# A two-layer hybrid trunk: SwiGLU in products of 256 columns, other TensorE work between k tiles, and attention's values moved beside the recurrence's products

## The chip, the cores and the metric

The kernel runs on one core of one Trainium2 chip. The metric is the device time of one launch in microseconds (us); the time before is the median of three runs. A profile of one execution is read beside it. Five engines work in parallel, each through its own queue in order: TensorE (PE in the profile; its weight loads are PEld), VectorE (DVE), ScalarE (ACT), GpSimd (POOL) and SyncE (SP, which only issues the transfers here).

## The reference, cut to what matters

Two layers, 256 tokens, width 1024, all in float32:

```
h = rms_norm(x, norm_mix);  z = h @ w_in        # 4768 columns, split in nine parts
y_a = latent attention(z parts) @ w_proj_a      # 8 heads, causal, two blocks of 128 queries
y_b = gated linear recurrence(z parts) @ w_proj_b   # 4 heads, 128 x 128
x = x + (sigmoid(g_a) * y_a + sigmoid(g_b) * y_b) @ w_out
h = rms_norm(x, norm_ffn)
x = x + (silu(h @ w_gate) * (h @ w_up)) @ w_down    # 2816 wide
```

## The kernel before, in words

The activations lie transposed: 128 channels in the partitions, 256 tokens along the columns. Each float32 operand of a large product is split in two parts of type float32r, a high one and the rest (`split`, L207). A product of two split operands is three products on TensorE: high by high, high by low, low by high (low by low is left out). A **k tile** is one slice of 128 of the sum, that is, three such products which add into one PSUM tile.

There are two ways to write a k tile. `mm3` (L217) issues three products of 256 columns, at L227 (weights' high part by the activations' high part), L228 and L229. SwiGLU uses `mmw` (L231): one product of 512 columns, the weights' high part by the activations' high and low part side by side (L235), and one of 256 columns, the weights' low part by the activations' high part (L236). `mmw` leaves two sums in the two halves of a PSUM tile, so ScalarE copies one half (L862) and VectorE adds the other (L863) before the row scale is multiplied in (L864). For each of the 22 tiles of SwiGLU's width there are 2 x 8 k tiles (gate and up), and for each of the 8 output tiles 22 k tiles (down): 528 k tiles a layer, 1056 in all.

The weights come in chunks of about 1 MB in the order of `chunk_plan` (L46). `load` (L105) issues the transfer from SP's queue, ScalarE rounds it to the high part (L118), VectorE or now and then GpSimd makes the low part (L120), two chunks ahead of use.

Attention's two generators and the recurrence give small products in plain float32: transposes of heads (L482), scores (L570), transposes of the probabilities (L591), values (L597), the recurrence's products (L674, L696, L712, L780) and its transposes (L724); the norms' sums over tokens (L257) and the row scales (L275) are plain float32 too. They are issued from generators: the loop at L799 to L804 calls `next(at, ...)` and `next(rec, None)` ahead of each chunk of the input projection. In the program as written, one call of `attention()` (L602) does the scores of one step and the transposes and values of the step before. The order on each engine is then made by a scheduler that simulates a timeline and takes, among instructions that are ready by it, those of higher priority first; so it can place a small product in the middle of another tile's k tile where the k tile's next product is, by its own clock, not first in line.

Of the kernel before, what the change touches and what calls it, by code (L numbers as in the profile page):

```python
# [9 lines left out]
F32 = mybir.dt.float32  # L10
# [5 lines left out]
ALU = mybir.AluOpType  # L16
AX = mybir.AxisListType

P = 128
T = 256  # L20
TT = T // P
D = 1024
KD = D // P
L = 2
NH, NOPE, ROPE, VD = 8, 64, 32, 64
# [57 lines left out]
def trunk(ctx: ExitStack, tc: tile.TileContext, x_in, w_in, vec_in, gqk_in, cst_in, msk_in, out):  # L83
    nc = tc.nc
    V, S, G, PE = nc.vector, nc.scalar, nc.gpsimd, nc.tensor
# [6 lines left out]
    acc = ctx.enter_context(tc.tile_pool(name="acc", bufs=2, space=bass.MemoryType.PSUM))  # L92
    prj = ctx.enter_context(tc.tile_pool(name="prj", bufs=2, space=bass.MemoryType.PSUM))
    trp = ctx.enter_context(tc.tile_pool(name="trp", bufs=2, space=bass.MemoryType.PSUM))
    hgp = ctx.enter_context(tc.tile_pool(name="hgp", bufs=2, space=bass.MemoryType.PSUM))
# [107 lines left out]
    def bc(ap, shape):  # L203
        return ap.broadcast_to(shape)
# [11 lines left out]
    def mm3(ps, pairs, late=False, opens=True, closes=True):  # L216
        n = len(pairs)  # L217
        if late:
            for i, ((ah, al), (bh, bl)) in enumerate(pairs):
                PE.matmul(ps, ah, bh, start=i == 0, stop=False)  # L220
                PE.matmul(ps, ah, bl, start=False, stop=False)
            for i, ((ah, al), (bh, bl)) in enumerate(pairs):
                PE.matmul(ps, al, bh, start=False, stop=i == n - 1)
            return
        shared = not (opens and closes)
        for i, ((ah, al), (bh, bl)) in enumerate(pairs):
            PE.matmul(ps, ah, bh, start=opens and i == 0, stop=False, skip_group_check=shared)  # L227
            PE.matmul(ps, ah, bl, start=False, stop=False, skip_group_check=shared)  # L228
            PE.matmul(ps, al, bh, start=False, stop=closes and i == n - 1, skip_group_check=shared)  # L229

    def mmw(ps, items):  # L231

        n = len(items)
        for i, ((ah, al), b) in enumerate(items):
            PE.matmul(ps, ah, b, start=i == 0, stop=False)  # L235
            PE.matmul(ps[:, 0], al, b[:, 0], start=False, stop=i == n - 1)  # L236

    def squares(src, kt, both=False):

# [43 lines left out]
    def norm_in(l, col):  # L283

        xx = lay.tile([P, KD, 2, T], F32R, name="xx")
        xh, xl = xx[:, :, 0], xx[:, :, 1]
        for k in range(KD):
            split(xh[:, k], xl[:, k], xT[:, k], vec[:, l, col + k:col + k + 1])
        r, _, ps = norm_rows(token_stats(xT, KD, both=True))
        return xx, xh, xl, r, norm_cols(ps)  # L290
# [25 lines left out]
    for l in range(L):  # L316
# [248 lines left out]
        def scores(t, h0, hb):  # L565
            ns = (t + 1) * P
            ps = prj.tile([P, 512], F32, name="prj")
            pv = ps.rearrange("p (h s) -> p h s", s=ns)
            for h in range(hb):
                PE.matmul(pv[:, h], qT[:, h0 + h, t * P:(t + 1) * P], kT[:, h0 + h, :ns], start=True, stop=True)  # L570
            V.tensor_tensor(pv[:, :, t * P:], pv[:, :, t * P:], bc(cmask.unsqueeze(1), [P, hb, P]), ALU.add)
            mx = wk.tile([P, 4], F32, name="mx")
            V.tensor_reduce(mx[:, :hb], pv, AX.X, ALU.max)
            nb = wk.tile([P, 4], F32, name="nb")
            V.tensor_tensor(nb[:, :hb], mx[:, :hb], nsc[:, t, h0:h0 + hb], ALU.mult)
            pr = wk.tile([P, 512], F32, name="pr")
            sm = wk.tile([P, 4], F32, name="sm")
            prv = pr.rearrange("p (h s) -> p h s", s=ns)
            for h in range(hb):
                S.activation(prv[:, h], pv[:, h], AF.Exp, bias=nb[:, h:h + 1], scale=sc[:, t, h0 + h:h0 + h + 1], accum_out=sm[:, h:h + 1])  # L580
            rs = wk.tile([P, 4], F32, name="rs")
            V.reciprocal(rs[:, :hb], sm[:, :hb])
            for h in range(hb):
                S.activation(prv[:, h], prv[:, h], AF.Identity, scale=rs[:, h:h + 1])
            return pr

        def values(t, h0, hb, pr, po):

            pt = trp.tile([P, 512], F32, name="trp")
            for c in range(4):  # L590
                PE.transpose(pt[:, c * P:(c + 1) * P], pr[:, c * P:(c + 1) * P], ident)  # L591
            pT = wk.tile([P, 4, P], F32, name="pT")
            S.copy(pT, pt.rearrange("p (c s) -> p c s", c=4))
            for h in range(0, hb, 2):
                for s in range(t + 1):
                    for u in range(2):
                        PE.matmul(po[u * VD:(u + 1) * VD, (h0 + h) // 2], av[:, s, h0 + h + u], pT[:, (h + u) * (t + 1) + s], start=s == 0, stop=s == t)  # L597

        def attn_out(t, po):
            split(ah[:, :, t * P:(t + 1) * P], al[:, :, t * P:(t + 1) * P], po)  # L600

        def attention():  # L602
            prev = None
            for t in range(TT):
                hb = 4 // (t + 1)
                po = None
                for h0 in range(0, NH, hb):
                    cur = (t, h0, hb, scores(t, h0, hb))
                    if prev:
                        values(*prev)  # L610
                        if prev[0] != t:
                            attn_out(prev[0], prev[4])
                    if po is None:
                        po = trp.tile([P, 512], F32, name="trp").rearrange("p (c s) -> p c s", c=4)
                    prev = cur + (po,)
                    yield
            values(*prev)
            attn_out(prev[0], prev[4])
            yield

# [167 lines left out]
        for ci in (3, 4):  # L790
# [3 lines left out]
            if ci == 4:  # L794
                next(at)
        tchunk(5)
        tchunk(6)
        next(at)
        for ci in [0] + list(range(7, 17)):  # L799
            if ci in (8, 10, 12, 14):  # L800
                next(at, None)
            next(rec, None)
            if ci == 0:
                hchunk(0)  # L804
            else:
                tchunk(ci)
            if ci == 8:
                for h in range(HH):
                    th = wk.tile([P, T], F32, tag="w1", bufs=3, name="thg")
                    S.activation(th, sg[:, h], AF.Tanh, scale=0.5)  # L810
                    V.scalar_tensor_tensor(sg[:, h], th, 1.0, sg[:, h], ALU.add, ALU.mult)
# [35 lines left out]


        xx, xh, xl, r, rb = norm_in(l, V_FFN)
        ffp = tc.alloc_tile_pool(name=f"ffn{l}", bufs=1)  # L850
        ff2 = ffp.tile([P, KF, 2, T], F32R, name="ff2")
        for m in range(KF):
            W = weights(l, f"gu{m}")
            if m % 2 == 0:
                pss = [acc.tile([P, 2, T], F32, name="acc"), trp.tile([P, 2, T], F32, name="trp")]
            else:
                pss = [hgp.tile([P, 2, T], F32, name="hgp"), prj.tile([P, 2, T], F32, name="prj")]
            g = ffp.tile([P, 2, T], F32, name="g", bufs=2)
            for j, ps in enumerate(pss):
                o = j * KD * P  # L860
                mmw(ps, [(W(o + k * P, P), xx[:, k]) for k in range(KD)])
                S.copy(g[:, j], ps[:, 1])  # L862
                V.tensor_tensor(g[:, j], g[:, j], ps[:, 0], ALU.add)  # L863
                (V, G)[j].tensor_tensor(g[:, j], g[:, j], rb, ALU.mult)  # L864
            th = ffp.tile([P, T], F32, name="th", bufs=2)
            S.activation(th, g[:, 0], AF.Tanh, scale=0.5)
            V.scalar_tensor_tensor(th, th, 1.0, g[:, 0], ALU.add, ALU.mult)  # L867
            hd = ffp.tile([P, T], F32, name="hd", bufs=2)
            G.tensor_tensor(hd, th, g[:, 1], ALU.mult)  # L869
            split(ff2[:, m, 0], ff2[:, m, 1], hd, 0.5)  # L870

        cur = None
        for m in range(KD):
            ps = acc.tile([P, 2, T], F32, name="acc")
            items = []
            for k in range(KF):
                i = m * KF + k
                if cur is None or cur[0] != i // 16:
                    cur = (i // 16, weights(l, f"dn{i // 16}"))
                items.append((cur[1]((i % 16) * P, P), ff2[:, k]))  # L880
            mmw(ps, items)
            for j in range(2):
                V.tensor_tensor(xT[:, m], xT[:, m], ps[:, j], ALU.add)
            if l == L - 1:
                nc.sync.dma_start(out[:, m], xT[:, m])
        ffp.release()
# [84 lines left out]
```

## Time and profile before

| | |
|---|---|
| median of 3 runs | 767.38 us (767.37 to 767.92) |
| the profiled execution's own time | 767.33 us |
| its span, first to last instruction | 765.5 us |
| PE busy | 758.3 us, 5676 products |
| PEld busy | 693.4 us |
| DVE / ACT / POOL busy | 584.9 / 443.7 / 259.5 us |
| granted TensorE clock | 0.999 of full speed |

The span has two equal layers. In the trace the first layer's SwiGLU runs from 200.1 to 387.5 us and the second's from 574.3 to 761.9. Products on PE overlap: a row's duration includes the pipeline, so the time that one takes from the next is the difference of two starts. That difference is called the pitch here.

### The profile page before, as it was taken

The page shows a single profiled execution, that of the slowest core. Times are in us where ns is not written, and L with a number is a line of the kernel's source. Part 1 is how long each engine was busy: PE and PEld are TensorE (multiplying, and loading weights), DVE is VectorE, ACT ScalarE, POOL GpSimd, SP SyncE. Part 2 cuts the span into 40 slices and gives each one's busy share as a digit, 9 for nine tenths or more (in the row PEclk, how much of TensorE's full clock was granted, in tenths as well). Part 3 has the DMA queues.
Part 4 walks back from the last instruction along what each step waited for, and adds up shares of the span by engine and source line. Part 5 has one row for each costly group of instructions (what it writes and reads, how often), then busy time and mean ns, then how long its engine had stood idle before and what let it go on. Part 6 is the DMA issues. An engine that isn't in the chain of part 4 may idle for free.

```text
span 765.5 us, 14316 instructions
## 1 busy us (share of the span) xinstructions
PE 758.3 (99%) x5676; PEld 693.4 (91%) x5676; DVE 584.9 (76%) x866; ACT 443.7 (58%) x811; POOL 259.5 (34%) x275
## 2 busy tenths in 40 slices
PE   9999999999999999999999999999999999999998
PEld 6899999999988888888899999999998888888886
DVE  6799876678898888866667988757888988887542
ACT  6668766545465556554447796654565655655330
POOL 0685422024333443411126823201432444443000
PEclk9999999999999999999999999999999999999999
DMA  7654434436565555555534544444465555646630
GB/s 280 221 175 166 166 116 161 166 116 212 168 220 176 209 170 202 180 185 199 196 118 166 181 154 167 134 143 165 167 221 168 188 195 174 211 166 200 206 124 21
DMA packets 20802, 133.07 MB, mean 174 GB/s; under 512 B 2432, under 2 KB 3712, under 8 KB 5504
## 3 DMA queue, kind: packets, MB, share of 16 engines
q1 hardware_dynamic: 20736, 132.17, 51.0%
q8 instruction: 44, 0.72, 0.4%
q14 instruction: 22, 0.18, 0.1%
HBM read 131.11 MB, written 1.05 MB: 173 GB/s over the span
## 4 chain that ended last, share of the span: by engine, by line
PE 93%; issue 2%; POOL 1%; DVE 1%; DMA 1%; ACT 1%; SPq 1%; POOLq 0%
PE acc L235 16%; PE acc L227 11%; PE acc L229 11%; PE acc L228 10%; PE acc L236 8%; PE hgp L235 5%; PE prj L235 5%; PE trp L235 5%; PE prj L236 3%; PE trp L236 3%; PE hgp L236 3%; PE prj L227 2%; PE prj L229 2%; PE prj L228 2%; PE prj L570 1%
## 5 line engine op out<-in xcount | busy, mean ns | idle before, releaser
L120 DVE TENSOR_TENSOR wl<-st,wh 128x1024 fp32r<-128x1024 f32 (+3 forms) x241 | 322.0, 1337 | 74.1 <-ACT wh L118 72.8
L118 ACT CAST wh<-st 128x1024 fp32r<-128x1024 f32 (+3 forms) x249 | 257.1, 1038 | 139.2 <-PE acc L235 64.3
L227 PE MATMUL acc<-xx,wh 128*128 128x256 f32 x472 | 133.5, 283 | 0.0
L229 PE MATMUL acc<-xx,wl 128*128 128x256 f32 x472 | 132.3, 281 | 0.3 <-DVE wl L120 0.3
L228 PE MATMUL acc<-xx,wh 128*128 128x256 f32 x472 | 132.2, 280 | 0.0
L235 PE MATMUL acc<-ff,wh 128*128 128x512 f32 x352 | 124.3, 397 | 0.0
L236 PE MATMUL acc<-ff,wl 128*128 128x256 f32 x352 | 98.6, 281 | 0.0
L229 PEld LDWEIGHTS acc<-xx,wl 128*128 128x128 f32 x472 | 88.9, 189 | 1.4 <-issue 0.9
L227 PEld LDWEIGHTS acc<-xx,wh 128*128 128x128 f32 x472 | 89.0, 188 | 0.8 <-issue 0.2
L228 PEld LDWEIGHTS acc<-xx,wh 128*128 128x128 f32 x472 | 88.9, 188 | 0.7 <-issue 0.7
L864 POOL TENSOR_TENSOR g<-g,rb 128x256 f32<-128x256 f32 x44 | 37.2, 846 | 135.5 <-DVE g L863 123.1
L235 PEld LDWEIGHTS acc<-ff,wh 128*128 128x128 f32 x352 | 66.0, 188 | 16.2
L869 POOL TENSOR_TENSOR hd<-th,g 128x256 f32<-128x256 f32 x44 | 66.1, 1504 | 7.4 <-DVE th L867 4.5
L213 ACT ACTIVATE ff<-hd 128x256 fp32r<-128x256 f32 x44 | 18.4, 419 | 84.6 <-POOL hd L869 84.6
L236 PEld LDWEIGHTS acc<-ff,wl 128*128 128x128 f32 x352 | 66.1, 188 | 0.2
L235 PE MATMUL prj<-xx,wh 128*128 128x512 f32 x176 | 63.5, 399 | 0.0
L235 PE MATMUL acc<-xx,wh 128*128 128x512 f32 x176 | 63.3, 397 | 0.0
L235 PE MATMUL hgp<-xx,wh 128*128 128x512 f32 x176 | 63.2, 397 | 0.0
L235 PE MATMUL trp<-xx,wh 128*128 128x512 f32 x176 | 63.1, 397 | 0.0
L250 POOL TENSOR_TENSOR sq<-sq 128x256 f32<-128x256 f32 x27 | 26.3, 974 | 88.5 <-ACT sq L244 53.9
L236 PE MATMUL acc<-xx,wl 128*128 128x256 f32 x176 | 49.6, 282 | 0.0
L236 PE MATMUL hgp<-xx,wl 128*128 128x256 f32 x176 | 49.5, 281 | 0.0
(259 smaller groups left out, 1732.1 us busy)
## 6 DMA issues: line engine op xcount, KB each, us to landing
st<-in_w_dram SPq DMA_DIRECT2D x115, 1024.0 KB, 4.8
st<-in_w_dram SPq DMA_DIRECT2D x4, 1088.0 KB, 5.0
st<-in_w_dram SPq DMA_DIRECT2D x4, 576.0 KB, 3.8
st<-in_w_dram SPq DMA_DIRECT2D x3, 512.0 KB, 6.8
xT<-in_x_dram SPq DMA_DIRECT2D x4, 256.0 KB, 5.5
out_dram<-xT SPq DMA_DIRECT2D x8, 128.0 KB, 1.9
st<-in_w_dram SPq DMA_DIRECT2D x2, 256.0 KB, 4.1
cst<-in_cst_dram SPq DMA_DIRECT2D x1, 260.0 KB, 7.6
```

The lines of the kernel that those rows point to most:

```text
L118: S.copy(wh[:, :n_], st[:, c:c + n_])
L120: eng.tensor_tensor(wl[:, :n_], st[:, c:c + n_], wh[:, :n_].bitcast(F32), ALU.subtract)
L213: S.activation(hi, src, AF.Copy if isinstance(scale, float) else AF.Identity, scale=scale)
L227: PE.matmul(ps, ah, bh, start=opens and i == 0, stop=False, skip_group_check=shared)
L228: PE.matmul(ps, ah, bl, start=False, stop=False, skip_group_check=shared)
L229: PE.matmul(ps, al, bh, start=False, stop=closes and i == n - 1, skip_group_check=shared)
L235: PE.matmul(ps, ah, b, start=i == 0, stop=False)
L236: PE.matmul(ps[:, 0], al, b[:, 0], start=False, stop=i == n - 1)
L250: G.tensor_tensor(tot, tot, sq, ALU.add)
L570: PE.matmul(pv[:, h], qT[:, h0 + h, t * P:(t + 1) * P], kT[:, h0 + h, :ns], start=True, stop=True)
L864: (V, G)[j].tensor_tensor(g[:, j], g[:, j], rb, ALU.mult)
L869: G.tensor_tensor(hd, th, g[:, 1], ALU.mult)
```

## The change

Three edits:

1. SwiGLU's gate, up and down use `mm3`; `mmw` is gone. Each gate and up pair is one PSUM tile from `acc` or `prj`, and one multiplication by the row scale of 512 columns takes the place of two copies, two additions and two multiplications. The down product has one addition into `xT` in place of two.
2. In `mm3`, the second and third product of a k tile are given a higher priority in the scheduler.
3. Attention's `values` is cut in two: `turned` (transposes and the copy out of PSUM) and, after a yield, `values`. The generator is called in more places: after `tchunk(5)`, and ahead of each of the chunks 7 to 15.

```diff
         for i, ((ah, al), (bh, bl)) in enumerate(pairs):
             PE.matmul(ps, ah, bh, start=opens and i == 0, stop=False, skip_group_check=shared)
-            PE.matmul(ps, ah, bl, start=False, stop=False, skip_group_check=shared)
-            PE.matmul(ps, al, bh, start=False, stop=closes and i == n - 1, skip_group_check=shared)
-
-    def mmw(ps, items):
...
+            with tc.high_priority():
+                PE.matmul(ps, ah, bl, start=False, stop=False, skip_group_check=shared)
+                PE.matmul(ps, al, bh, start=False, stop=closes and i == n - 1, skip_group_check=shared)
...
-        def values(t, h0, hb, pr, po):
+        def turned(pr):
 
             pt = trp.tile([P, 512], F32, name="trp")
             for c in range(4):
                 PE.transpose(pt[:, c * P:(c + 1) * P], pr[:, c * P:(c + 1) * P], ident)
             pT = wk.tile([P, 4, P], F32, name="pT")
             S.copy(pT, pt.rearrange("p (c s) -> p c s", c=4))
+            return pT
+
+        def values(t, h0, hb, pT, po):
+
...
+            for step in [(t, h0, 4 // (t + 1)) for t in range(TT) for h0 in range(0, NH, 4 // (t + 1))] + [None]:
+                pr = scores(*step) if step else None
+                if prev:
+                    (t, h0, hb), pT = prev[0], turned(prev[1])
+                    yield
...
+                    values(t, h0, hb, pT, po)
+                    if not step or step[0] != t:
+                        attn_out(t, po)
+                        po = None
+                prev = (step, pr)
+                yield
...
         tchunk(5)
+        next(at)
         tchunk(6)
         next(at)
         for ci in [0] + list(range(7, 17)):
-            if ci in (8, 10, 12, 14):
+            if ci in range(7, 16):
                 next(at, None)
...
-            if m % 2 == 0:
-                pss = [acc.tile([P, 2, T], F32, name="acc"), trp.tile([P, 2, T], F32, name="trp")]
-            else:
-                pss = [hgp.tile([P, 2, T], F32, name="hgp"), prj.tile([P, 2, T], F32, name="prj")]
+            ps = (acc, prj)[m % 2].tile([P, 2, T], F32, name=("acc", "prj")[m % 2])
+            for j in range(2):
+                o = j * KD * P
+                mm3(ps[:, j], [(W(o + k * P, P), xs[k]) for k in range(KD)])
             g = ffp.tile([P, 2, T], F32, name="g", bufs=2)
-            for j, ps in enumerate(pss):
-                o = j * KD * P
-                mmw(ps, [(W(o + k * P, P), xx[:, k]) for k in range(KD)])
-                S.copy(g[:, j], ps[:, 1])
-                V.tensor_tensor(g[:, j], g[:, j], ps[:, 0], ALU.add)
-                (V, G)[j].tensor_tensor(g[:, j], g[:, j], rb, ALU.mult)
+            V.tensor_tensor(g, ps, bc(rb.unsqueeze(1), [P, 2, T]), ALU.mult)
...
-            mmw(ps, items)
-            for j in range(2):
-                V.tensor_tensor(xT[:, m], xT[:, m], ps[:, j], ALU.add)
+            mm3(ps[:, 0], items)
+            V.tensor_tensor(xT[:, m], xT[:, m], ps[:, 0], ALU.add)
```

In the changed file the three products of `mm3` stand at L227, L230 and L231, the sums over tokens at L252, the row scales at L270, the heads' transposes at L477, the scores at L565, the probabilities' transposes at L586, the values at L596 and the recurrence's products at L671, L693, L709 and L777.

TensorE's order at the start of SwiGLU in the first layer, around the row scales of its norm (`prj<-dg,cst`). Before:

```order
L235 MATMUL acc<-xx,wh 128x512
L236 MATMUL acc<-xx,wl 128x256
L275 MATMUL prj<-dg,cst 128x256
L235 MATMUL prj<-xx,wh 128x512
L236 MATMUL prj<-xx,wl 128x256
```

And in the changed kernel:

```order
L227 MATMUL acc<-xx,wh 128x256
L230 MATMUL acc<-xx,wh 128x256
L231 MATMUL acc<-xx,wl 128x256
L227 MATMUL acc<-xx,wh 128x256
L230 MATMUL acc<-xx,wh 128x256
L270 MATMUL prj<-dg,cst 128x256
L227 MATMUL prj<-xx,wh 128x256
L230 MATMUL prj<-xx,wh 128x256
L231 MATMUL prj<-xx,wl 128x256
```

A k tile of two products is now one of three of 256 columns, and after the row scales the stream goes on with the first product of a k tile. Nothing but products of 256 columns follows there until the next layer's norm.

TensorE's order in the input projection, where one step's values (`trp<-pT,av`) and the recurrence's third set of products (`hgp<-rows,hf`) stand, the first layer. Before, the values are alone between two k tiles, and the recurrence's products follow six k tiles later (the rows between are left out):

```order
L228 MATMUL acc<-xx,wh 128x256
L229 MATMUL acc<-xx,wl 128x256
L597 MATMUL trp<-pT,av 64x128 x4
L227 MATMUL acc<-xx,wh 128x256
L228 MATMUL acc<-xx,wh 128x256
```

And in the changed kernel they stand together:

```order
L230 MATMUL acc<-xx,wh 128x256
L231 MATMUL acc<-xx,wl 128x256
L596 MATMUL trp<-pT,av 64x128 x4
L671 MATMUL hgp<-rows_1306,hf 32x48 x8
L671 MATMUL hgp<-rows_1308,hf 32x48 x8
L671 MATMUL hgp<-rows_1310,hf 32x48 x8
L671 MATMUL hgp<-rows_1312,hf 32x48 x8
L227 MATMUL acc<-xx,wh 128x256
```

What were two places where small products stand between the large ones is one. Over the whole program, from the opening's first large product on, there were 63 such places and are 53. Before, 29 of the 63 stood ahead of a second or third product of a k tile; now four do.

## Rows read from the trace of the kernel before

**Rows 1.** The page's first part: busy time, share of the span, instructions of each engine.
```profile
PE 758.3 (99%) x5676; PEld 693.4 (91%) x5676; DVE 584.9 (76%) x866; ACT 443.7 (58%) x811; POOL 259.5 (34%) x275
```
**Rows 2.** Who PE waited for, longest first: total us, times, longest us.
```profile
PE trp L482 <- DVE kh L512: 0.9, 1, 0.9
```
**Rows 3.** Stretch of `proj` and `out`, L227 alone: stretch, PE busy (count), PEld, clock.
```profile
160.00:200.00 40.00, 31.63 (x118) 21.64 (x118) 1.00 0.55 186
```
**Rows 4.** A stretch of SwiGLU's gate and up, L235 alone: the same columns.
```profile
225.00:320.00 95.00, 95.00 (x270) 50.53 (x270) 1.00 0.56 189
```
**Rows 5.** PE's timeline where `out` ends and SwiGLU begins: start us, duration us, instruction.
```profile
199.44 0.28 PE L227 MATMUL acc<-yh,wh 128*128 128x256 f32 x1
...
200.12 0.39 PE L235 MATMUL acc<-xx,wh 128*128 128x512 f32 x1
200.34 0.28 PE L236 MATMUL acc<-xx,wl 128*128 128x256 f32 x1
```
**Rows 6.** PE's timeline after SwiGLU: the next layer's first 21 products.
```profile
387.50 0.28 PE L227 MATMUL acc<-xx,wh 128*128 128x256 f32 x1
...
389.98 0.28 PE L227 MATMUL hgp<-xx,wh 128*128 128x256 f32 x1
```
**Rows 7.** PE's timeline around 64 of the recurrence's products, resumed at L227.
```profile
98.51 0.28 PE L229 MATMUL acc<-xx,wl 128*128 128x256 f32 x1
98.72 0.89 PE L674 MATMUL hgp<-rows,hf 128*32 128x48 f32 x64
99.54 0.38 PE L227 MATMUL acc<-xx,wh 128*128 128x256 f32 x1
99.76 0.28 PE L228 MATMUL acc<-xx,wh 128*128 128x256 f32 x1
...
100.21 0.28 PE L229 MATMUL acc<-xx,wl 128*128 128x256 f32 x1
```
**Rows 8.** PE's timeline after one step's values, standing alone, resumed at L227.
```profile
95.82 0.66 PE L597 MATMUL trp<-pT,av 128*64 128x128 f32 x8
96.41 0.38 PE L227 MATMUL acc<-xx,wh 128*128 128x256 f32 x1
96.63 0.28 PE L228 MATMUL acc<-xx,wh 128*128 128x256 f32 x1
...
96.98 0.28 PE L228 MATMUL acc<-xx,wh 128*128 128x256 f32 x1
```
**Rows 9.** PE's timeline after transposes of heads, resumed at L228.
```profile
430.04 0.36 PE L228 MATMUL acc<-xx,wh 128*128 128x256 f32 x1
430.24 0.28 PE L229 MATMUL acc<-xx,wl 128*128 128x256 f32 x1
...
430.60 0.28 PE L229 MATMUL acc<-xx,wl 128*128 128x256 f32 x1
```
**Rows 10.** PE's timeline around the row scales of the second layer's first norm.
```profile
398.44 0.59 PE L275 MATMUL prj<-dg,cst 128*128 128x256 f32 x2
398.68 0.47 PE L229 MATMUL hgp<-xx,wl 128*128 128x256 f32 x1
...
399.22 0.28 PE L229 MATMUL hgp<-xx,wl 128*128 128x256 f32 x1
...
399.79 0.28 PE L228 MATMUL hgp<-xx,wh 128*128 128x256 f32 x1
```
**Rows 11.** Groups by line: form, count, busy us, mean ns, idle before.
```profile
L228 PE MATMUL acc<-xx,wh 128*128 128x256 f32 x472 | 132.2, 280 | 0.0
...
L227 PE MATMUL acc<-yh,wh 128*128 128x256 f32 x128 | 35.0, 276 | 0.0
```
**Rows 12.** Groups by line on DVE: the weights' low part; a row scale over 512 columns.
```profile
L120 DVE TENSOR_TENSOR wl<-st,wh 128x1024 fp32r<-128x1024 f32 (+3 forms) x241 | 322.0, 1337 | 74.1 <-ACT wh L118 72.8
...
L395 DVE TENSOR_TENSOR gs<-acc,rb 128x512 f32<-128x512 f32 x16 | 11.0, 686 | 2.7 <-PE acc L229 2.7
```
**Rows 13.** The timeline's end: the last additions into `xT`.
```profile
761.91 0.87 DVE L883 TENSOR_TENSOR xT<-xT,acc 128x256 f32<-128x256 f32 x2 [6.90 <-PE acc L236]
```

More of the change, by code (lines that the diff above doesn't have):

```diff
@@ L227, in mm3 @@
             PE.matmul(ps, ah, bh, start=opens and i == 0, stop=False, skip_group_check=shared)
-            PE.matmul(ps, ah, bl, start=False, stop=False, skip_group_check=shared)
-            PE.matmul(ps, al, bh, start=False, stop=closes and i == n - 1, skip_group_check=shared)
-    def mmw(ps, items):
[L233 to L236, printed above, removed]
+            with tc.high_priority():
+                PE.matmul(ps, ah, bl, start=False, stop=False, skip_group_check=shared)
+                PE.matmul(ps, al, bh, start=False, stop=closes and i == n - 1, skip_group_check=shared)
     def squares(src, kt, both=False):
@@ L602, in attention @@
         def attention():
[L603 to L612, printed above, removed]
+            prev, po = None, None
+            for step in [(t, h0, 4 // (t + 1)) for t in range(TT) for h0 in range(0, NH, 4 // (t + 1))] + [None]:
[3 more added lines that the diff above has]
+                    yield
                     if po is None:
                         po = trp.tile([P, 512], F32, name="trp").rearrange("p (c s) -> p c s", c=4)
[L615 to L619, printed above, removed]
+                    values(t, h0, hb, pT, po)
[4 more added lines that the diff above has]
+                yield
         kk = hf
@@ L849, in trunk @@
         xx, xh, xl, r, rb = norm_in(l, V_FFN)
+        xs = [(xh[:, k], xl[:, k]) for k in range(KD)]
         ffp = tc.alloc_tile_pool(name=f"ffn{l}", bufs=1)
@@ L879, in trunk @@
                     cur = (i // 16, weights(l, f"dn{i // 16}"))
-                items.append((cur[1]((i % 16) * P, P), ff2[:, k]))
-            mmw(ps, items)
-            for j in range(2):
-                V.tensor_tensor(xT[:, m], xT[:, m], ps[:, j], ALU.add)
+                items.append((cur[1]((i % 16) * P, P), (ff2[:, k, 0], ff2[:, k, 1])))
+            mm3(ps[:, 0], items)
+            V.tensor_tensor(xT[:, m], xT[:, m], ps[:, 0], ALU.add)
             if l == L - 1:
```

## Prediction

> **What bounds the kernel now.** I began with the page's first part: PE is busy for 99% of the span, and no other engine for more than 76%, weight loads apart [rows 1]. The waits come next. Once the opening is over, the longest wait of a product for another engine is 0.9 us, once [rows 2]. So the time is the sum of PE's pitches, and an edit counts only where it changes how many products there are, how closely they follow one another, or what PE waits for. A product's duration doesn't tell that, since products overlap; the difference of two starts does.
>
> So I read pitches, and they show the thing on which all else rests: the same 256-column product runs at one of two pitches. In `proj` and `out`, 40 us hold 118 products of L227, one to a k tile, so a k tile takes 40/118 = 0.339 us, 0.113 us a product [rows 3]. The last six products ahead of SwiGLU take 200.12 - 199.44 = 0.68 us, again 0.113 [rows 5]. In SwiGLU, 95 us hold 270 k tiles: 0.352 us each [rows 4]. That k tile streams 512 + 256 columns, as many as three products of 256, so it runs at 0.117 to 0.118 us for 256 columns. I call 0.113 the quick pitch and 0.118 the slow one; the clock is 1.00 in both stretches.
>
> The slow pitch does not belong to the 512-column form as such. The first such product, straight after `out`, takes 200.34 - 200.12 = 0.22 us, two quick pitches [rows 5]; then SwiGLU falls to the slow pitch. And the next layer's first 21 products, of 256 columns, go on slowly: 387.50 to 389.98 us is 2.48/21 = 0.118 [rows 6]. So the pitch is kept from product to product until something changes it. Mixing 512 with 256 columns makes it slow; products of 256 columns keep what they have. In both layers `proj` and `out` keep the quick pitch for over 350 products on end.
>
> What changes it otherwise is a small float32 product in between. After 64 of the recurrence's products the stream resumes at L227 and is quick: 99.76 to 100.21 us, four products in 0.45 [rows 7]. After the heads' transposes it resumes at L228, a k tile's second product, and is slow: 430.24 to 430.60, three in 0.36 [rows 9]. Over the timeline I counted what follows such a place, outside SwiGLU: resumed at the first product, 17 of 21 are quick; at the second, 2 of 10; at the third, 4 of 12. One of the four exceptions is a step's values standing alone [rows 8].
>
> **The change part by part.** *SwiGLU's products.* 1056 k tiles change from two products to three. In columns nothing changes; the cost is one more weight load each, and `proj` and `out` show three loads and three products in 0.339 us, so the load is hidden there. If the stream is quick, a k tile goes from 0.352 to 0.339: 0.013 x 1056 = 13.7 us. If it stays slow, 0. These are the two ends. I take the quick one, for this reason: `out` hands over a quick stream, and in each layer only two things stand in SwiGLU's way, the norm's sums and its row scales. The first resume at L230, the second product, so I expect some 10 slow k tiles there (0.1 us a layer). The row scales follow and resume at L227. Their only instance within 256-column products resumes after a first step of 0.31 us and is then quick: 399.22 to 399.79, five in 0.57 [rows 10]. After that nothing comes in between for the rest of the layer. I count 13.5 us.
>
> The Trainium skill speaks against this edit (TensorE: Matmul & The Clock Gate, "Back-to-back issue gap"): the gap is N/2.4 + 2.5 ns, a fixed cost per product that favours wide ones. By it, two products of 256 cost 2.5 ns more than one of 512, an estimate of 1056 x 2.5 ns = 2.6 us lost. The trace has neither of its gaps (109 and 216 ns): quick it shows 113 and some 220, slow 118 and some 235, the wide one twice the narrow one in both.
>
> *The rest of SwiGLU.* Per pair of tiles two copies, two additions and two multiplications go, and one multiplication over 512 columns comes, shown at 686 ns [rows 12]. I cost it at nothing: PE doesn't wait for these engines, and they get less work. PSUM tiles come from two pools in place of four, but one tile now holds a pair, so the pairs ahead are four as before. If that cover went, each of the 44 pairs could cost up to 0.69 us, 30 us; I hold it for remote, since the slot is needed again only four pairs, some 20 us, later.
>
> *The low parts.* Raised priority means that PE's queue holds L231 right behind its k tile, so a low part (L120, 1.34 us [rows 12]) that is late now stops PE where other products were taken before. The bounds are 0 and a whole 1.34 us at each half chunk; I take 0, as `proj` and `out` already run in this order at the same 0.339 us a k tile without a stop.
>
> *Fewer interruptions.* There are 10 places fewer. One costs, beside its own products, the step into it, 98.72 - 98.51 = 0.21 in place of 0.11, and the step out, 99.76 - 99.54 = 0.22 in place of 0.11 [rows 7]: 0.2 us. Ten give 2.0 us; the bounds are 1 (transposes go in without the first step) and 3.
>
> *Resuming at the first product.* In the input projection, L228 has a mean duration of 280 ns against 276 for `out`'s quick ones [rows 11]; I counted some 680 of its 1416 products as slow, so 680 x 0.0045 = 3.0 us could go. By 17 in 21 against 23 in 43 over all places, about half goes: 1.5 us, bounds 0 and 3.0.
>
> *Values a chunk later.* The same products are issued, so this is only the order already counted. The copy of the transposes has a whole chunk more, and `ah` is needed only by `proj`, over a chunk after the last values.
>
> *The end.* The last two additions take 0.87 us after PE is done [rows 13]; one goes: 0.4 us.
>
> The sum is 13.5 + 2.0 + 1.5 + 0.4 = 17.4 us. The profiled execution took 767.33 us, 0.05 under the median, so 767.38 - 17.4 = 750.0 us.
>
> **The rivals.** (1) *SwiGLU stays slow.* The row scales may leave the stream slow, or 1056 more weight loads may. For it: slow streams of 256 columns do persist [rows 6], and only one instance of the row scales is there. Against it: that instance. The other terms remain: 767.4 - 3.9 = 763.5 us.
>
> (2) *Quick for a part.* One layer only, or a fall midway. No quick stream of 256 columns fell without a small product in between, but the longest seen is some 360 products and SwiGLU has 1584 a layer. Half of 13.5 is lost: 756.8 us.
>
> (3) *A fixed cost per product.* The stream stays slow and each of the 1056 added products costs a little besides. The rows bound it by the difference between two quick 256-column products, 0.227, and the quick 512-column one, 0.22 [rows 5], under 7 ns; at the middle, 3.5 ns, it is 3.7 us, and 763.5 + 3.7 = 767.2 us, no change. The gap of the Trainium skill's page TensorE: Matmul & The Clock Gate, named above, is this rival's rule.
>
> (4) *PE stops for low parts.* The raised products stand at the head of PE's queue while the weights' low part is being made. It decides from 17.4/1.34 = 13 half chunks that each wait a whole low part; at 20 of them 750.0 + 27 = 777 us, slower. For it: VectorE is the busiest of the others. Against it: [rows 2], and that VectorE loses work in SwiGLU.
>
> **How the numbers follow.** The forecast has 0.68, its own range 746.5 to 753.5 from the bounds above; (2) 0.14, (1) 0.11, (3) 0.04, (4) 0.03. A measurement of this kernel can tell about 0.2% (1.5 us) from no change. The forecast, (1) and (2) are faster by more than that: 0.93; (3) is the same: 0.04; (4) slower: 0.03. The range of 8 in 10 takes in (2) and leaves (1), (3) and (4) out: 745.5 to 762.
>
> **What would show it.** Right: SwiGLU's stretch 6 to 7 us shorter in each layer, L227 there at 0.339 us from one to the next, durations near 276 ns, and the recurrence's stretches 1 us shorter each. Wrong: durations of 281 ns through SwiGLU (1), a change from 276 to 281 within it (2), or waits of PE for L120 of more than an occasional 0.3 us (4). If the row scales leave a slow stream in both layers, the forecast is wrong by some 13 us.

## The result, and the profile after

The changed kernel takes 756.44 us, the median of four runs (756.26 to 757.00); the kernel before, on the same chip, 767.40 us (767.37 to 767.92). The ratio is 0.9856, with a 95% interval of 0.9843 to 0.9868. So 11.0 us are gone, where the forecast had 17.4. The profiled execution took 757.00 us, with a span of 754.7.

The table is made from the trace's starts on PE: each stretch runs from its first large product to that of the next (layer 0's first row from the first product of all, the last row from the last product's start). The third column is all_mended, an experiment told of below.

| us | before | after | all_mended |
|---|---|---|---|
| layer 0, opening and input projection | 154.93 | 154.89 | 153.79 |
| layer 1, input projection | 142.82 | 142.02 | 142.00 |
| `proj`, both layers | 44.44 | 44.42 | 44.42 |
| `out`, both layers | 43.58 | 44.13 | 44.13 |
| SwiGLU, layer 0 / layer 1 | 187.38 / 187.26 | 182.30 / 182.30 | 180.57 / 180.46 |
| from the last product's start | 3.9 | 3.4 | 3.4 |

SwiGLU gave 10.0 us, the rest 0.8. The opening, from the first product to the first one of L227, took 0.9 us longer in this execution (23.9 us). Over all traces of this study it lies between 22.3 and 24.8 us; in pool_hgp and flip, which differ from the changed kernel in SwiGLU alone, it takes 22.8 and 24.5.

The page's first part answers to [rows 1]. PE has 1056 products more and 13 us less to do:

```profile
PE 745.3 (99%) x6732; PEld 728.8 (97%) x6732; DVE 536.8 (71%) x762; ACT 421.8 (56%) x723; POOL 191.5 (25%) x231
```

The same stretch of gate and up as in [rows 4], now of L227 alone (stretch, PE busy and count, PEld, clock, DMA share, GB/s), and the groups by line that answer to [rows 11] (count, busy us, mean ns, idle before):

```profile
225.00:320.00 95.00, 77.14 (x280) 52.39 (x280) 1.00 0.58 195
```
```profile
L230 PE MATMUL prj<-xx,wh 128*128 128x256 f32 x352 | 97.2, 276 | 0.0
L230 PE MATMUL acc<-ff,wh 128*128 128x256 f32 x352 | 96.8, 276 | 0.0
```

280 k tiles take 95 us, 0.339 each against 0.352 before, at the same granted clock; and the mean durations are 276 ns. SwiGLU runs at the quick pitch. By the starts it does so for 1557 products on end in layer 0 and 1506 in layer 1, to the last one. The next layer's first products, slow in [rows 6], now inherit the quick pitch: 21 of them from 385.71 to 388.09 us, 0.113 each.

PE's timeline at the row scales, after [rows 10] and where the forecast hung:

```profile
210.95 0.28 PE L230 MATMUL acc<-xx,wh 128*128 128x256 f32 x1
211.07 0.59 PE L270 MATMUL prj<-dg,cst 128*128 128x256 f32 x2
211.31 0.47 PE L227 MATMUL prj<-xx,wh 128*128 128x256 f32 x1
211.62 0.28 PE L230 MATMUL prj<-xx,wh 128*128 128x256 f32 x1
...
211.86 0.28 PE L227 MATMUL prj<-xx,wh 128*128 128x256 f32 x1
211.97 0.28 PE L230 MATMUL prj<-xx,wh 128*128 128x256 f32 x1
```

The step into the row scales is 0.12 us, the slow pitch; from 211.86 on it is 0.11. Where then are the missing us? The view of waits, as in [rows 2], has these rows (total us, times, longest); before, PE waited for a low part of weights once, 0.3 us, and never for `xT`:

```profile
PE acc L231 <- DVE wl L120: 1.9, 3, 0.9
...
PE acc L227 <- DVE xT L842: 0.4, 2, 0.2
```

PE's timeline where SwiGLU starts, which answers to [rows 5], and DVE's beside it:

```profile
202.28 0.28 PE L231 MATMUL acc<-xx,wl 128*128 128x256 f32 x1
202.77 0.36 PE L227 MATMUL acc<-xx,wh 128*128 128x256 f32 x1 [0.22 <-DVE xT L842]
202.97 0.28 PE L230 MATMUL acc<-xx,wh 128*128 128x256 f32 x1
203.22 0.38 PE L227 MATMUL acc<-xx,wh 128*128 128x256 f32 x1
204.35 0.39 PE L231 MATMUL acc<-xx,wl 128*128 128x256 f32 x1 [0.74 <-DVE wl L120]
204.57 0.28 PE L227 MATMUL acc<-xx,wh 128*128 128x256 f32 x1
```
```profile
201.95 0.67 DVE L842 TENSOR_TENSOR xT<-xT,acc 128x512 f32<-128x512 f32 x1
...
203.07 1.22 DVE L120 TENSOR_TENSOR wl<-st,wh 128x1024 fp32r<-128x1024 f32 x1
```

From 202.28 to 204.57 PE starts five products in place of twenty. The stretch costs 1.7 us in layer 0 and 1.8 in layer 1. PE's order in the program, with buffer numbers, says which tiles these products work on: `acc_2757` is the first pair of gate and up, `acc_2893` the third, in the slot that `out`'s last tile leaves.

```
L231 MATMUL acc_2757<-xx_2689,wl_2631 128x256
L227 MATMUL acc_2893<-xx_2689,wh_2817 128x256
L230 MATMUL acc_2893<-xx_2689,wh_2817 128x256
L227 MATMUL acc_2757<-xx_2689,wh_2630 128x256
L231 MATMUL acc_2893<-xx_2689,wl_2818 128x256
L227 MATMUL acc_2893<-xx_2689,wh_2817 128x256
```

The first pair's gate has used the activations that are ready (six of eight slices; the last two come out of `out`'s last addition, L842). Then PE's queue holds the third pair, whose slot is free only behind that same addition, and whose low part (`wl_2818`, L120) VectorE makes from 203.07 to 204.29. The second pair, whose weights are there, isn't used: it lies in `prj`, and in the order nothing of it stands ahead of the row scales, which take a tile of the same pool before it. The two tiles lie in different banks of PSUM, so it isn't a full slot that holds the pair back; that the order in which a pool's tiles are taken does so is argued, and pool_hgp below shows only that in another pool the pair runs there. Before, the second pair's gate lay in `hgp` and filled this time. The first pair's second half, its up part, didn't fill it either: it stands behind the gate. No run moves it.

A second new stop stands in `out`, PE's timeline and VectorE's, and below them the same place before:

```profile
183.84 0.28 PE L227 MATMUL acc<-yh,wh 128*128 128x256 f32 x1
184.14 0.50 PE L230 MATMUL acc<-yl,wh 128*128 128x256 f32 x2
```
```profile
183.68 0.75 DVE L214 SCALAR_TENSOR_TENSOR yl<-y,yh 128x256 fp32r<-128x256 f32 x2
```
```profile
183.88 0.28 PE L227 MATMUL acc<-yh,wh 128*128 128x256 f32 x1
184.00 0.29 PE L228 MATMUL acc<-yl,wh 128*128 128x256 f32 x1
```
```profile
183.44 0.75 DVE L214 SCALAR_TENSOR_TENSOR yl<-y,yh 128x256 fp32r<-128x256 f32 x2
```

A step of 0.30 where the same place, the 51st product of `out`, had 0.12 before: the product waits for the merged activations' low part, which VectorE makes at 183.68 behind a low part of weights (L120, 181.99, 1.76 us). `out` begins at 178.29 here and at 178.33 before, so VectorE begins it 5.38 us behind that start in place of 5.11 (from the starts in ns). `out` is longer by the same 0.27 us, in each layer.

The end answers to [rows 13]: one addition.

```profile
751.56 0.42 DVE L876 TENSOR_TENSOR xT<-xT,acc 128x256 f32<-128x256 f32 x1 [7.06 <-PE acc L231]
```

### The profile page after: what moved, and what is told of

It reads as the page before. It is cut to its first block, busy times and chain, and to the rows that moved or that the text cites. A ratio compares the mean times of both kernels' runs of the same rounds, so it can differ in the third digit from the quotient of the medians.

```text
span 754.7 us, 16131 instructions
## 1 busy us (share of the span) xinstructions
PE 745.3 (99%) x6732; PEld 728.8 (97%) x6732; DVE 536.8 (71%) x762; ACT 421.8 (56%) x723; POOL 191.5 (25%) x231
## 4 chain that ended last, share of the span: by engine, by line
PE 88%; DVE 5%; issue 3%; POOL 1%; DMA 1%; ACT 1%; SPq 1%; POOLq 0%; DVEq 0%
PE acc L227 20%; PE acc L231 20%; PE acc L230 20%; PE prj L227 7%; PE prj L231 7%; PE prj L230 7%; DVE wl L120 2%; PE prj L565 1%; DVE xx L214 1%; DMA cst<-in_cst_dram 1%; PE trp L596 1%; PE trp L477 1%; PE trp L586 1%; PE hgp L671 1%; DVE xT L842 1%
## 5 line engine op out<-in xcount | busy, mean ns | idle before, releaser
L120 DVE TENSOR_TENSOR wl<-st,wh 128x1024 fp32r<-128x1024 f32 (+3 forms) x241 | 295.5, 1228 | 138.3 <-ACT wh L118 137.7
L227 PE MATMUL acc<-xx,wh 128*128 128x256 f32 x824 | 232.0, 282 | 0.4 <-DVE xT L842 0.4
L231 PE MATMUL acc<-xx,wl 128*128 128x256 f32 x824 | 228.2, 278 | 1.9 <-DVE wl L120 1.9
L230 PE MATMUL acc<-xx,wh 128*128 128x256 f32 x824 | 228.3, 278 | 0.0
L227 PEld LDWEIGHTS acc<-xx,wh 128*128 128x128 f32 x824 | 155.1, 188 | 1.9 <-issue 0.9
L231 PEld LDWEIGHTS acc<-xx,wl 128*128 128x128 f32 x824 | 154.5, 188 | 2.5 <-DVE wl L120 2.5
L230 PEld LDWEIGHTS acc<-xx,wh 128*128 128x128 f32 x824 | 154.7, 188 | 0.0
L227 PE MATMUL prj<-xx,wh 128*128 128x256 f32 x352 | 97.5, 277 | 0.0
L230 PE MATMUL prj<-xx,wh 128*128 128x256 f32 x352 | 97.2, 276 | 0.0
L231 PE MATMUL prj<-xx,wl 128*128 128x256 f32 x352 | 97.2, 276 | 0.0
L231 PE MATMUL acc<-ff,wl 128*128 128x256 f32 x352 | 96.8, 276 | 0.0
L227 PE MATMUL acc<-ff,wh 128*128 128x256 f32 x352 | 96.8, 276 | 0.0
L230 PE MATMUL acc<-ff,wh 128*128 128x256 f32 x352 | 96.8, 276 | 0.0
L227 PEld LDWEIGHTS prj<-xx,wh 128*128 128x128 f32 x352 | 66.1, 188 | 0.1
L230 PEld LDWEIGHTS prj<-xx,wh 128*128 128x128 f32 x352 | 66.1, 188 | 0.1
L231 PEld LDWEIGHTS prj<-xx,wl 128*128 128x128 f32 x352 | 66.1, 188 | 0.0
L231 PEld LDWEIGHTS acc<-ff,wl 128*128 128x128 f32 x352 | 65.9, 188 | 0.0
L230 PEld LDWEIGHTS acc<-ff,wh 128*128 128x128 f32 x352 | 65.9, 188 | 0.0
L227 PEld LDWEIGHTS acc<-ff,wh 128*128 128x128 f32 x352 | 65.9, 188 | 0.0
```

The lines of the kernel that those rows point to most:

```text
L120: eng.tensor_tensor(wl[:, :n_], st[:, c:c + n_], wh[:, :n_].bitcast(F32), ALU.subtract)
```

## The experiments

Nine kernels ran. Each time stands beside runs of the kernel before on the same chip. Edit 1 is SwiGLU, edit 2 the raised priority, edit 3 the values and the places where attention's generator is called.

**swiglu_alone**: edit 1 alone, on the kernel before; the lines are shown against the changed kernel.

```diff
-            with tc.high_priority():
-                PE.matmul(ps, ah, bl, ...)
-                PE.matmul(ps, al, bh, ...)
+            PE.matmul(ps, ah, bl, ...)
+            PE.matmul(ps, al, bh, ...)
...   # attention's generator and its calls as before
```

> SwiGLU in products of 256 columns, with the order of the other work as before. Theory: the quick pitch is worth 13.8 us over 1056 k tiles, and the stop of 1.7 us a layer at SwiGLU's start belongs to this edit (a pair's two halves share one PSUM tile, and the second pair's pool waits for the row scales), not to the raised priority. So 767.4 - 13.8 + 3.5 - 0.4 = 756.7 us if the row scales leave a quick stream, with gaps of some 0.5 and 1.1 us near the start of SwiGLU. Rival: the stop comes from the raised priority, then there is none and the time is 753 us. Second rival: without the rule on k tiles the row scales leave a slow stream, then 767 to 770 us.

758.03 us (757.28 to 759.77), ratio 0.9884 (0.987 to 0.9899). SwiGLU is quick for 1557 and 1506 products, as in the changed kernel. The stop at its start is there too, without raised priority (PE's timeline):

```profile
203.32 0.31 PE L227 MATMUL acc<-xx,wh 128*128 128x256 f32 x1
204.36 0.39 PE L229 MATMUL acc<-xx,wl 128*128 128x256 f32 x1 [0.73 <-DVE wl L120]
```

So edit 1 brings both the gain and the stop. In layer 0, `out` is 0.6 us longer than before (22.41 us): behind a step of 0.13 at the place shown above its stream is slow.

**rest_alone**: edits 2 and 3, with SwiGLU as before; the lines are shown against the changed kernel.

```diff
-                mm3(ps[:, j], [(W(o + k * P, P), xs[k]) for k in range(KD)])
+                mmw(ps, [(W(o + k * P, P), xx[:, k]) for k in range(KD)])
...   # with its four pools, copies and additions
```

> The raised priority and the values a chunk later, with SwiGLU as before. Theory, from the sums over the two traces: steps into and out of the small products' places fall by some 1.2 us, slow products outside SwiGLU by only 0.3, and the stop in out costs 0.5: 766 to 767 us, at most 0.2% faster. Rival, the prediction's terms: 2.0 + 1.5 = 3.5 us faster, 764 us.

767.20 us (766.29 to 768.50), ratio 0.9998 (0.9988 to 1.0007): nothing. The trace shows a gain and its loss. The input projections are 1.5 us shorter; `out` takes 22.68 us in place of 21.79 in both layers. In layer 1:

```profile
556.87 0.28 PE L227 MATMUL acc<-yh,wh 128*128 128x256 f32 x1
557.17 0.50 PE L230 MATMUL acc<-yl,wh 128*128 128x256 f32 x2
...
558.57 0.28 PE L230 MATMUL acc<-yl,wh 128*128 128x256 f32 x1
558.69 0.28 PE L231 MATMUL acc<-yh,wl 128*128 128x256 f32 x1
```

The stop of 0.30 us is there, and behind it the stream is slow (0.12 a product) to `out`'s end, which is 0.6 us. In the changed kernel the same stop left it quick.

**prio_only**: edit 2 alone, on the kernel before.

```diff
+            with tc.high_priority():
                 PE.matmul(ps, ah, bl, ...)
                 PE.matmul(ps, al, bh, ...)
```

> The kernel before with the raised priority alone. Theory: the priority puts small products between k tiles, but what they leave depends on their shape and on a phase of a few ns, not on the k tile's place; slow products outside SwiGLU stay at 650 to 750 of those of 256 columns, out gains a stop of 0.3 us a layer: 767 to 768.5 us, same. Rival, the prediction's term: half of the slow products outside SwiGLU go, 766 us or less.

767.65 us (767.24 to 768.61), ratio 0.9998 (0.9989 to 1.0007). `out` takes 22.06 and 22.07 us, with the stop, as in the changed kernel: the stop comes with the raised priority. The input projections are 0.4 us shorter in sum, and the slow ones among their products of 256 columns fall only from 649 to 617, so the prediction's 1.5 us isn't in edit 2 alone.

**pool_hgp**: the changed kernel with the odd pairs in another pool.

```diff
-            ps = (acc, prj)[m % 2].tile([P, 2, T], F32, name=("acc", "prj")[m % 2])
+            ps = (acc, hgp)[m % 2].tile([P, 2, T], F32, name=("acc", "hgp")[m % 2])
```

> The changed kernel with SwiGLU's odd pairs in PSUM pool hgp in place of prj. Theory: TensorE stops 1.7 us a layer at SwiGLU's start because the first pair needs the last two channel tiles of the norm's input, its up half cannot begin while the gate half is open in the same PSUM tile, and the second pair's pool is held for the row scales. With hgp the second pair's gate can run there: 756.4 - 3.4 = 753.0 us, and no gap over 0.3 us from 200 to 206 us. Rival: VectorE is late with the weights' low part in any order; then the stop moves and the time stays within 1 us of 756.4.

Four runs: 752.63, 759.83, 767.67 and 767.81 us, at a granted clock of 1.00 each. The stop is gone: gate and up of layer 0 take 120.72 us in place of 122.46. But the time falls on three levels some 7 us apart, and the trace of the run of 759.83 shows what they are. L227 in gate and up (layer 0) and in layer 1:

```profile
225.00:320.00 95.00, 77.08 (x281) 52.49 (x280) 1.00 0.55 194
640.00:735.00 95.00, 75.42 (x269) 50.38 (x270) 1.00 0.53 185
```

281 k tiles against 269 in the same 95 us: layer 0 is quick, layer 1 slow, for all of its 1498 products. The row scales set it. In layer 1 they left the stream slow:

```profile
577.05 0.59 PE L270 MATMUL prj<-dg,cst 128*128 128x256 f32 x2
...
577.71 0.28 PE L231 MATMUL hgp<-xx,wl 128*128 128x256 f32 x1
577.83 0.28 PE L227 MATMUL hgp<-xx,wh 128*128 128x256 f32 x1
```

One instruction, the row scales of layer 1, decided 6.8 us (SwiGLU takes 180.6 us in layer 0 and 187.3 in layer 1). That the other three runs are both layers quick (752.63) and none (767.67, 767.81) is read from the levels; they have no trace.

**flip**: the changed kernel with one product of 512 columns into an unused tile ahead of the seventh pair, in both layers, and in layer 1 one float32 product of 256 columns ahead of the fifteenth.

```diff
+            if m == 6:
...   # wide is a new tile from trp
+                PE.matmul(wide, W(0, P)[0], xx[:, 0], start=True, stop=True)
+            if m == 14 and l == 1:
...   # small is another
+                PE.matmul(small[:, :T], ones, rb, start=True, stop=True)
```

> The changed kernel with one more product of 512 columns ahead of SwiGLU's seventh pair in both layers (its result is not used), and in the second layer a float32 product of 256 columns like the row scales ahead of the fifteenth pair (not used either). Theory, that the pitch is kept until something changes it: in the first layer the pitch is 0.118 from the seventh pair to the end, some 16 of 22 pairs and all of down, 432 k tiles x 0.013 = 5.6 us lost; in the second it is slow from the seventh to the fourteenth pair, 128 k tiles or 1.7 us, and quick again after. Together some 7.5 us: 764 us. Rival: a wide product costs its own 0.24 us and the pitch is set by the shape of the stream, not by its past: 757 us, 0.113 throughout.

766.48 us, one run. PE's timeline at the two places, layer 0 and layer 1:

```profile
236.28 0.28 PE L231 MATMUL prj<-xx,wl 128*128 128x256 f32 x1
236.39 0.39 PE L856 MATMUL trp<-xx,wh 128*128 128x512 f32 x1
236.62 0.28 PE L227 MATMUL acc<-xx,wh 128*128 128x256 f32 x1
236.73 0.28 PE L230 MATMUL acc<-xx,wh 128*128 128x256 f32 x1
...
237.09 0.28 PE L230 MATMUL acc<-xx,wh 128*128 128x256 f32 x1
...
656.85 0.59 PE L859 MATMUL trp<-rb,cst 128*128 128x256 f32 x2
...
657.64 0.28 PE L227 MATMUL acc<-xx,wh 128*128 128x256 f32 x1
657.75 0.28 PE L230 MATMUL acc<-xx,wh 128*128 128x256 f32 x1
```

Three steps from 236.73 on take 0.36 us; the step from 657.64 on takes 0.11. Layer 0 is quick for 212 products, and after the single wide one slow for 1347, to the layer's end and into the next. Layer 1 is quick for 212, slow for 384, and after the float32 product quick for 908. Everything else there is the same work. The pitch is a state that the stream keeps: what SwiGLU's 528 k tiles of a layer cost is decided at the last place ahead of them where something else stands.

**wide_only**: the kernel before with SwiGLU's low product over all 512 columns too, so that wide products alone stand there; its sums have a term (low by low) that the kernel's products leave out elsewhere.

```diff
-            PE.matmul(ps[:, 0], al, b[:, 0], start=False, stop=i == n - 1)
+            PE.matmul(ps, al, b, start=False, stop=i == n - 1)
```

> The kernel before with the low product of SwiGLU also over 512 columns (low by low added, which the kernel leaves out elsewhere): every product of SwiGLU is 512 wide. Theory A, that mixing widths makes the stream slow: equal widths keep the quick pitch, 0.226 us a product, and SwiGLU takes 1056 x 0.453 = 478 us, in all 767.4 + 1056 x (0.453 - 0.353) = 873 us. Theory B, that a wide product makes it slow by itself: 0.235 us a product, 767.4 + 1056 x 0.117 = 891 us.

887.28 us, one run, against 767.89 for the kernel before. Divided by 1056, that is 0.113 us more per k tile for 256 columns more. PE's timeline in gate and up:

```profile
229.91 0.40 PE L235 MATMUL prj<-xx,wh 128*128 128x512 f32 x1
...
231.31 0.40 PE L235 MATMUL acc<-xx,wh 128*128 128x512 f32 x1
```

Six steps take 1.40 us. They alternate between 0.236 and 0.231, 0.233 on average: for 512 columns the slow pitch is 0.235 (the kernel before), the quick one 0.226 (the first such product behind `out`). So a stream of nothing but 512-column products didn't keep the quick pitch either. The prediction put the slow pitch down to the mixing of widths; mixing isn't needed for it.

**all_mended**: the changed kernel with the odd pairs in `hgp`, the row scales as two float32 products of 128 columns, and no raised priority in `out`.

```diff
-        PE.matmul(ps[:, :T], ones, dg.rearrange("p t c -> p (t c)"), start=True, stop=True)
+        for t in range(TT):
+            PE.matmul(ps[:, t * P:(t + 1) * P], ones, dg[:, t], start=True, stop=True)
...   # the pool as in pool_hgp; no raised priority in out
```

> The changed kernel with three edits: SwiGLU's odd pairs in pool hgp, the norms' row scales as two float32 products of 128 columns in place of one of 256, and no raised priority in out. Theory: in the traces so far a slow stream is quick after small products whose last has 128x128 elements in 22 of 22 cases, and after the 256-column row scales in only 11 of 15; the norm's sums always leave a slow stream ahead of the row scales. So SwiGLU is quick in both layers in every run: 756.4 - 3.4 (the stop at SwiGLU's start) - 0.6 (the stop in out) = 752.4 us, with runs within 1 us of each other. Rival: what the row scales leave is chance of the phase alone, whatever their shape; then some runs lie at 759 and 766 as for the kernel with hgp alone.

752.32 us (752.25 to 753.01), ratio 0.98 (0.9787 to 0.9814): the best of the study, 15.6 us under the kernel before on the same chip, where the changed kernel was 11.0 under it. PE's timeline over the start and over the row scales:

```profile
203.00 0.28 PE L227 MATMUL acc<-xx,wh 128*128 128x256 f32 x1
203.11 0.28 PE L227 MATMUL hgp<-xx,wh 128*128 128x256 f32 x1
203.22 0.28 PE L230 MATMUL hgp<-xx,wh 128*128 128x256 f32 x1
...
209.37 0.61 PE L271 MATMUL prj<-dg,cst 128*128 128x128 f32 x4
...
210.06 0.28 PE L231 MATMUL hgp<-xx,wl 128*128 128x256 f32 x1
210.17 0.28 PE L227 MATMUL hgp<-xx,wh 128*128 128x256 f32 x1
```

The second pair fills the start, without a stop, and the stream is quick behind the row scales in both layers. The four runs lie within 0.8 us of one another, and those of the next two kernels, which keep this pool and these row scales, within 2.1 and 0.8: the levels of pool_hgp don't come back. Gate and up take 120.73 us in each, 1.7 and 1.8 less than in the changed kernel. The stop in `out` stayed, though the raised priority is gone there.

**swiglu_mended**: swiglu_alone with the pool and the row scales of all_mended.

> SwiGLU in products of 256 columns alone, the order of the other work as before, with pool hgp and the row scales in two products of 128 columns. Theory: quick in both layers: 767.4 - 13.8 - 0.4 = 753.2 us; the raised priority and the later values are worth the rest to the kernel with all three, some 0.8 us. Rival: they are worth the 2.0 + 1.5 us of the prediction; then this one is 3.5 us slower than that one, 756 us.

754.86 us (754.17 to 756.25), ratio 0.9829 (0.9815 to 0.9842). What edits 2 and 3 add is thus 2.5 us, between the two expectations. By the starts 1.6 of it is the input projections' and 0.4 lies in `out` and at SwiGLU's start, where layer 1's stream was slow in this kernel; 0.3 more lies behind the last product, and the rest isn't settled.

**merge_free**: all_mended with the raised priority taken out of `proj` as well as `out`.

```diff
-                    mm3(pss[c][:, s], [... for k in range(4)])
+                    mm3(pss[c][:, s], [... for k in range(4)], first=False)
...   # the same in out
```

> The kernel of all_mended without the raised priority in proj as well as in out; nothing is left out of the computation. Theory: the stop of 0.29 us at out's start, and the slow k tile behind it, come from the order in which the products stand when proj ends, so with the order free TensorE takes other products meanwhile, and the time is 0.6 us under all_mended: 751.7 us. Rival: the wait is for VectorE, which makes the low part of the merged activations only behind a 1.8 us low part of weights, whatever TensorE's order: the stop stays and the time is that of all_mended, 752.3 us.

752.56 us (752.40 to 753.21): no change. The times are the rival's, but the trace is the theory's in part. The stop is gone in both layers; layer 1's `out` takes 21.80 us. In layer 0, however, the longest step left is this one:

```profile
183.13 0.28 PE L227 MATMUL acc<-yh,wh 128*128 128x256 f32 x1
183.25 0.29 PE L230 MATMUL acc<-yl,wh 128*128 128x256 f32 x1
183.38 0.28 PE L231 MATMUL acc<-yh,wl 128*128 128x256 f32 x1
```

A step of 0.13 us, and behind it 141 products are slow: 0.6 us in `out`, and 0.2 more in SwiGLU up to the row scales. The stop's 0.3 us came back as pitch. So the stop comes with the raised priority in `proj`, and not by the order of the products in `out`: the one that waits is the 51st with it and without it. What moves is VectorE. In the six traces with that priority it begins the low part 5.38 us behind `out`'s start, in the five without it 5.11, in both layers; why the priority makes it later isn't followed up. The stop would be worth taking away only together with whatever then sets the pitch.

## Why the prediction was right or wrong

**SwiGLU's products: right.** 13.5 us was the term. Where nothing else disturbs SwiGLU (all_mended), it is 6.81 + 6.80 = 13.6 us under the kernel before. The mechanism, a pitch that is handed on and kept, is shown by flip. The sign that was named for it, SwiGLU 6 to 7 us shorter in each layer, came only there and in the other kernels without the stop at SwiGLU's start; in the changed kernel it is 5.1 and 5.0. Rival (1) and rival (3) fell for this kernel: three products of 256 columns take 0.339 us, three times the quick pitch, and a quick wide product takes as long as two quick narrow ones (0.226 and 2 x 0.113), so an added product costs nothing that can be seen. The fixed cost per product of the Trainium skill (TensorE: Matmul & The Clock Gate, "Back-to-back issue gap"), which that section gives for an isolated product, would have shown between these two; no run here shows it.

**But its ground was thinner than the chance of 0.68 said.** The row scales' one instance in the trace of before was taken as a rule. Over ten traces (all but wide_only's) a float32 product of 256 columns, the row scales or flip's inserted one, left 11 streams quick and 5 slow, and pool_hgp, which differs by a pool, has both outcomes in one run. Rival (1) named this; that the changed kernel fell on the good side of it was luck as far as the prediction goes. Three of the four kernels that keep the 256-column row scales with SwiGLU in three products had every traced layer quick: what makes pool_hgp's differ is open but for what the last section finds.

**The rest of SwiGLU: wrong, and this is the step that failed.** It was costed at nothing because "one tile now holds a pair, so the pairs ahead are four as before". The count of tiles was right; the count of pairs that can run at the start wasn't. Of the four slots only the first pair's was of use there: the other one of `acc` was behind `out`'s last addition, and those of `prj` came behind the row scales in the order. The price is 1.74 + 1.85 = 3.6 us, shown by pool_hgp, where the pool alone takes it away (layer 0), and by all_mended (both layers). The wait is one for a low part of weights, which rival (4) had as its mechanism, but raised priority isn't its cause: swiglu_alone has it without. That rival's sign, waits of PE for L120 of more than 0.3 us, showed (0.7 and 0.9 us, once a layer).

**Resuming at the first product: wrong.** 1.5 us was the term, and of 2.7 us that the slow pitch costs by the starts in the two layers' input projections (behind the opening and behind layer 1's norm) 0.1 went. The order did what was said (of the 43 places behind the opening where a stream of 256 columns resumes, 39 resume at the first product), but of these 24 are quick and 12 slow, with three too short to tell: 2 in 3, not 17 in 21. The count of the trace of before mixed the k tile's place with which small products stood there. Sorted by the last small product instead, over the same ten traces, it reads otherwise: behind 128x128 float32 products a slow stream became quick 43 times in 45, though a quick one fell 19 times in 81; behind the norm's sums (128x1) the stream was slow 23 times in 24, whatever it had been.

**Fewer interruptions: right in kind, 1.3 of 2.0 us.** In the input projections the steps into the places and the first steps behind them exceed the quick pitch by 9.7 us before and 8.4 after. The 0.2 us a place took every place to have a long step at both ends; many have one only.

**The low parts: 0 was taken, 0.55 came**, the two stops in `out`. "`proj` and `out` already run in this order" was the wrong cover: the product that waits has the same place in `out` as before, but raised priority in `proj` comes with a VectorE that is 0.27 us later. merge_free shows that this priority makes the stop, though taking it away won nothing.

**The end**: 0.5 us (3.9 to 3.4), of which the addition is the 0.4 that was said.

In sum: 13.6 - 3.6 (start) - 0.55 (`out`) + 1.6 (input projections) + 0.2 (the products ahead of layer 1's norm, which inherit the quick pitch) + 0.5 = 11.75 us; the profiled execution gave 10.8 with an opening that was 0.9 longer. The forecast's 750.0 missed by 6.4 us: 3.6 are SwiGLU's start, 2.15 the small terms (3.9 were counted, 1.75 are left with `out`'s stops), and the rest lies within what the opening varies by. The time lies outside the forecast's own range, which ended at 753.5; the range of 8 in 10 holds it because that took in rival (2). It lies beside that rival's 756.8, but no part of SwiGLU fell back to the slow pitch; the agreement is by chance.

## What to carry to other kernels

Where one engine is busy for 99% of the span, measure the step from one start to the next, not the duration; where the same work shows two steps, ask which instruction ahead of it decides, and try that with one inserted instruction before a sum is built on a single instance. When tiles move to other pools, count not the slots but the tiles that can start at the moment when the engine has nothing else, and name what holds each. And a stop removed is a gain only once what follows it has been read: in merge_free's layer 0 it came back as pitch.

## What the runs showed of the hardware that was not expected

A stream of float32r products of 256 columns runs at 113.3 or at 117.7 ns a product, both at a granted clock of 1.00, and keeps either for as long as nothing else comes between (1557 products at the one, 1498 at the other). One 512-column product of the same type turned it slow, both times that it was tried in a quick stream; one float32 product of 256 columns turned it quick in flip; small waits (a step of 0.13 us in merge_free, of 0.30 in rest_alone) turned it slow, while the same 0.30 in the changed kernel and 0.13 in the kernel before did not. Which small product leaves which pitch is a statistic here, not a mechanism.

The traces hold one thing more, read after the experiments and tried by none of them: the outcome goes with the step into the small product. Over all eleven traces a float32 product of 256 columns that started 117 to 119 ns behind the last large one left a slow stream quick, 12 times in 12; where it started 121 or 122 ns behind, the stream stayed slow, 5 times in 5. Behind 128x128 float32 products a quick stream stayed quick where the step into the place was 116 to 120 ns (70 in 70) and fell where it was 205 or 206 (19 in 19). Starts are read to 1 ns, and many of these are the same place in another kernel's trace, so this is a lead and no more: why there are two pitches, and what a few ns decide, stays open.
